# Output projection in seven products: the bank for the products of block sums comes from another pair of places

## The chip, the cores and the metric

The kernel runs on one core of one Trainium2 chip. The metric is the device time of one execution in microseconds (us), lower being better. Engines are named as in the profile: PE is TensorE (PEld its weight loads), DVE is VectorE, ACT is ScalarE, POOL is GpSimd and SP is SyncE, which here only issues transfers.

## The reference

One layer of a hybrid encoder on 256 tokens of width 2048. Eight heads do softmax attention with forget gates (group A), eight do stick-breaking attention (group B). Each group's output is normalised over its 1024 columns, both are multiplied by `w_out` and added to the input, and a convolutional feed-forward follows. The change lies in the product with `w_out`:

```
D_MODEL = 2048; SEQ = 256; HEAD_DIM = 128; N_HEADS_FOX = N_HEADS_SB = 8
def hybrid_mixer(h, ...):
    proj = h @ w_in_l
    ...
    out_a = forgetting_attention(qa, ka, to_heads(va, N_HEADS_FOX), c)
    out_b = stick_breaking_attention(...)
    merged = jnp.concatenate([rms_norm(from_heads(out_a), out_norm_fox_l),
                              rms_norm(from_heads(out_b), out_norm_sb_l)], axis=-1)
    return merged @ w_out_l

def reference(...):
    h = rms_norm(x, attn_norm);  x = x + hybrid_mixer(h, ...)
    h = rms_norm(x, ffn_norm);   x = x + conv_ffn(h, ...)
```

## The kernel before

**Precision and splits.** All large products are made of float32 operands that are split into a high and a low part. `split` (L220, L221) does it for weights: ACT casts the raw 128x2048 tile into `w_hi`, and DVE subtracts to get `w_lo`. A product is then high x high, high x low and low x high: `in_three` (L245) issues, for one bank and four blocks of 128 rows, eight matmuls with `w_hi` and then four with `w_lo`. `w_hi` and `w_lo` have two buffers each in this stage, the raw tiles three, so that the split for a product waits until PE is through with the product two before it, and the load of a raw tile until the split of the tile three before it is done.

**The output projection.** For 256 tokens it makes two kinds of products. `token_major` makes plain ones for both halves of the tokens together: an `acc` tile of two banks, with 16 matmuls of `w_hi` and 8 of `w_lo` for each load of weights. For the heads of group A and the last 1024 columns, `in_seven` makes a 2x2 block product in seven products rather than eight, from sums of blocks of the operand (`oT_blocks`, split into `oT_sums`) and sums of blocks of the weights (`w_sum` and `x12`, to which POOL's transfers add other blocks in memory, L848). `in_seven` is a generator: `token_major` takes one step of it after each of its loads, so that on PE plain products alternate with products of the seven.

**Banks.** The seven products land in three accumulators: `bank_a` (products 1, 5, 6, 7), `bank_c` (product 2) and `bank_b` (products 3 and 4). After each product `residual` (L833) multiplies the bank by a factor for each token and adds it to the running `x` on DVE. PSUM places come from pools. `pss` has two places with tag "s", which the heads used for scores and transposed weights (`ps_s`, `ps_z`, `ps_p`). `psb` has two places with tag "t", which hold the heads' products with the values (`ps_o`), the sums over heads (`pg`, L919) and the transposes of the next stage (`ps_x`, L146). `psa` has the two `acc` tiles. With `bank_a` in use until the seventh product, `bank_b` gets the place that `bank_c` had.

**Order.** PE's instructions stand in program order. Those of DVE, ACT, POOL and SP are ordered by a scheduler, which follows the dependences and the priorities that the code gives; each engine then runs its list in that order.

The stage of interest lies between 325 and 400 us of the profiled execution. Its products on PE, in order, are called here: K1 (plain, group B, first columns, first half), B1 (`bank_b`, first of two), K2 (plain, second half), B2 (`bank_b`, second), `pg`, K3 (plain, next columns), A1 (`bank_a` from `w_sum`).

Of the kernel before, what the change touches and what calls it, by code (L numbers as in the profile page):

```python
# [9 lines left out]
F32 = mybir.dt.float32  # L10
# [5 lines left out]
P = 128  # L16
# [30 lines left out]
def hybrid_layer(  # L47
# [29 lines left out]
    psb = ctx.enter_context(tc.tile_pool(name="psb", bufs=2, space=bass.MemoryType.PSUM))  # L77
# [135 lines left out]
    def split(raw, a, b):  # L213
        hi = whi.tile([P, 2048], F32R, name="w_hi", tag="w_hi")
        lo = wlo.tile([P, 2048], F32R, name="w_lo", tag="w_lo")
        n = a * b
        with ExitStack() as turn:
            for ins in in_turn:
                turn.enter_context(tc.issue_after(ins.ins))
            last = [act.copy(hi[:, :n], raw[:, :n])]  # L220
            last.append(dve.tensor_tensor(lo[:, :n], raw[:, :n], f32(hi[:, :n]), op=ALU.subtract))  # L221
        last_split[:] = last
        if in_turn:
            in_turn[:] = last
        return (
            hi[:, :n].rearrange("p (a b) -> p a b", a=a),
            lo[:, :n].rearrange("p (a b) -> p a b", a=a),
        )

    def weights(src, a, b):  # L230
        with tc.high_priority(offset=AHEAD):
            return split(load(src), a, b)

    def rows_of(w, k0, n, c0, cols):
        return w[k0 * P : (k0 + n) * P, c0 : c0 + cols].rearrange("(k p) c -> p k c", p=P)

    def in_three(accs, parts, n, lhs, starts, stops, more=False):

        hi, lo = parts
        order = [(i, l, hi) for i in range(n) for l in range(2)] + [(i, 0, lo) for i in range(n)]
        for j, (i, l, r) in enumerate(order):
            for t, o in enumerate(accs):
                nc.tensor.matmul(  # L245
                    o, lhs(i, l, t), r[:, i, :], start=starts and j == 0,
                    stop=stops and j == 3 * n - 1, skip_group_check=more,
                )

    def of_half(h, part, t):  # L250
        return h[:, part, t * P : (t + 1) * P]
# [52 lines left out]
    with ExitStack() as actx:  # L304

        at = actx.enter_context(tc.tile_pool(name="at", bufs=1))
        pss = actx.enter_context(tc.tile_pool(name="pss", bufs=2, space=bass.MemoryType.PSUM))
# [487 lines left out]
        def block_parts():  # L795
            sums.extend(big.tile([P, NH, S], F32R, name="oT_sums", tag=f"hT{g}") for g in (1, 2))
            places = [[t[:, 4 * h : 4 * h + 4] for t in sums] for h in range(2)]
            for (hi, _), block in zip(places, blocks):
                in_order(act.copy(hi, block))
            for (hi, lo), block in zip(places, blocks):  # L800
                in_order(dve.tensor_tensor(lo, block, f32(hi), op=ALU.subtract))
# [29 lines left out]
        def residual(t, c, ps, factor):  # L831
            xs = xt[t][:, c : c + 512]
            dve.scalar_tensor_tensor(xs, ps, factor[:, t : t + 1], xs, op0=ALU.mult, op1=ALU.add)  # L833

        def in_seven(c0, plus_rg, minus_rg):

            w11, w12, w21, w22 = (rows_of(wo, 4 * h, 4, c0 + 512 * i, 512) for h in range(2) for i in range(2))
            banks = {}

            def of_heads(h, t):  # L840
                return lambda i, part, _: of_half(oT[4 * h + i], part, t)

            def of_sums(h, t):
                return lambda i, part, _: sums[part][:, 4 * h + i, t * P : (t + 1) * P]

            def plus(into, src):
                with tc.high_priority(offset=AHEAD):
                    nc.gpsimd.dma_start(  # L848
                        into.rearrange("p (a b) -> p a b", a=4), src, accum_op=ALU.add
                    )  # L850

            def product(bank, lhs, parts, to, factor=plus_rg):
                new = bank not in banks
                if new:
                    banks[bank] = pss.tile([P, 512], F32, name=bank, tag="s")
                in_three([banks[bank]], parts, 4, lhs, new, True, more=not new)
                residual(to[0], c0 + 512 * to[1], banks[bank], factor)

            w, x12 = (
                pool.tile([P, 2048], F32, name=name, tag=tag)  # L860
                for pool, name, tag in ((at, "w_sum", "vA"), (big, "x12", "hT0"))
            )
            with tc.high_priority(offset=AHEAD):
                for into, src in ((w, w11), (x12, w12)):
                    nc.sync.dma_start(into.rearrange("p (a b) -> p a b", a=4), src)
            yield
            yield
            yield
            with tc.issue_after(last_head[0].ins), tc.issue_after(last_head[1].ins):
                parts = split(w, 4, 512)  # L870
                in_order(dve.tensor_tensor(w, w, x12, op=ALU.add))
                block_parts()
            product("bank_a", of_heads(0, 0), parts, (0, 0))
            product("bank_c", of_heads(1, 0), weights(w21, 4, 512), (0, 0))
            yield
            with tc.high_priority(offset=AHEAD):
                parts = split(w, 4, 512)
            plus(w, w22)
            plus(x12, w22)
            product("bank_b", of_sums(0, 1), parts, (1, 1))  # L880
            yield
            product("bank_b", of_sums(1, 0), weights(w22, 4, 512), (0, 1))
            yield
            with tc.high_priority(offset=AHEAD):
                parts = split(w, 4, 512)
            plus(w, w21)
            product("bank_a", of_sums(1, 1), parts, (0, 1), minus_rg)
            yield
            with tc.high_priority(offset=AHEAD):
                parts = split(x12, 4, 512)  # L890
            product("bank_a", of_sums(0, 0), parts, (1, 1), minus_rg)
            yield
            with tc.high_priority(offset=AHEAD):
                parts = split(w, 4, 512)
            product("bank_a", of_heads(1, 1), parts, (1, 0))
# [405 lines left out]
```

## Time and profile before

| | |
|---|---|
| median of 3 runs | 1106.46 us (1105.9 to 1107.39) |
| the profiled execution's own time | 1107.04 us |
| its span | 1105.2 us |
| PE busy | 1096.8 us, 99% of the span |
| DVE / ACT / POOL busy | 895.3 / 709.0 / 47.9 us |
| mean granted clock of TensorE | 0.997 |
| moved by DMA | 249.04 MB, mean 225 GB/s |

The span runs from the first to the last instruction of the program; the execution takes 1.84 us beyond it. The chain that ended last is PE for 99% of the span. Busy time on PE counts matmuls at whatever clock was granted, so a stretch at half clock counts as busy and takes twice as long.

### The profile page before, as it was taken

How to read it: one execution, taken by the hardware profiler on the slowest of the kernel's cores; microseconds unless marked ns; L12 is line 12 of the kernel's file. 1: busy time of each engine (PE TensorE's matmuls, PEld its weight loads, DVE VectorE, ACT ScalarE, POOL GpSimd, SP SyncE). 2: the span in 40 equal slices, each digit the busy share in tenths (PEclk: the TensorE clock that was granted, in tenths of full speed). 3: DMA queues.
4: the chain of work that ended last, by engine and by line, in shares of the span. 5: the costliest groups of instructions: out<-in, count | busy, mean ns of one | idle time of the engine just before them, and what ended most of it. 6: DMA issues, size and time to landing. Idle time of an engine off the chain costs nothing.

```text
span 1105.2 us, 14835 instructions
## 1 busy us (share of the span) xinstructions
PE 1096.8 (99%) x5856; PEld 950.9 (86%) x5856; DVE 895.3 (81%) x957; ACT 709.0 (64%) x884; POOL 47.9 (4%) x49
## 2 busy tenths in 40 slices
PE   9999999999998999999999999999999999999998
PEld 7998888888887888888888888888888888888887
DVE  6656778877787777689889888889798888889896
ACT  6544555764673667677767776667676777577753
POOL 0000000000000000000000010100000010100010
PEclk9999999999998999999999999999999999999999
DMA  8776554676648495557989597986979689987975
GB/s 288 185 232 231 186 153 152 195 239 205 205 126 250 114 306 196 191 189 189 308 205 327 191 225 259 267 261 183 313 212 302 214 223 283 237 261 204 323 203 181
DMA packets 180991, 249.04 MB, mean 225 GB/s; under 512 B 4480, under 2 KB 119066, under 8 KB 180666
## 3 DMA queue, kind: packets, MB, share of 16 engines
q1 hardware_dynamic: 162458, 209.67, 57.7%
q0 software_dynamic: 18144, 37.89, 18.2%
q8 instruction: 46, 0.75, 0.3%
q10 hardware_dynamic: 320, 0.53, 0.1%
q14 instruction: 23, 0.19, 0.0%
HBM read 245.97 MB, written 2.11 MB: 224 GB/s over the span
## 4 chain that ended last, share of the span: by engine, by line
PE 99%; DVE 0%; DMA 0%; issue 0%; SPq 0%
PE pu L271 34%; PE acc L245 20%; PE pu L277 18%; PE bank_a L245 11%; PE bank_b L245 6%; PE bank_c L245 3%; PE acc L446 2%; PE acc L1179 1%; PE ps_x L146 1%; PE ps_o L612 1%; PE bank_a L1179 1%; PE ps_p L628 0%; DMA w_raw<-in_w_in_dram 0%; PE ps_o L613 0%; PE ps_h L324 0%; PE ps_s L540 0%
## 5 line engine op out<-in xcount | busy, mean ns | idle before, releaser
L221 DVE TENSOR_TENSOR w_lo<-w_raw,w_hi 128x2048 fp32r<-128x2048 f32 (+1 forms) x194 | 434.9, 2245 | 123.0 <-ACT w_hi L220 122.1
L220 ACT CAST w_hi<-w_raw 128x2048 fp32r<-128x2048 f32 (+1 forms) x194 | 363.5, 1876 | 229.3 <-PE acc L245 63.4
L271 PE MATMUL pu<-hT,w_hi 128*128 128x512 f32 x1664 | 394.0, 390 | 0.0
L271 PEld LDWEIGHTS pu<-hT,w_hi 128*128 128x128 f32 x1664 | 310.3, 188 | 63.1
L277 PEld LDWEIGHTS pu<-hT,w_lo 128*128 128x128 f32 x1664 | 211.9, 191 | 7.0
L277 PE MATMUL pu<-hT,w_lo 128*128 128x256 f32 x1664 | 215.2, 283 | 0.0
L245 PE MATMUL acc<-w_hi,hT 128*128 128x512 f32 (+1 forms) x576 | 124.5, 368 | 0.0
L245 PEld LDWEIGHTS acc<-w_hi,hT 128*128 128x128 f32 x576 | 101.9, 188 | 14.6
L221 DVE TENSOR_TENSOR w_lo<-w_sum,w_hi 128x2048 fp32r<-128x2048 f32 x34 | 77.8, 2290 | 21.6 <-ACT w_hi L220 21.6
L220 ACT CAST w_hi<-w_sum 128x2048 fp32r<-128x2048 f32 x34 | 64.9, 1909 | 44.8 <-PE pu L271 36.7
L996 ACT ACTIVATE tap<-up,ccol 128x256 f32<-128x256 f32 x176 | 74.6, 495 | 0.0
L245 PE MATMUL acc<-w_lo,hT 128*128 128x512 f32 (+1 forms) x288 | 64.6, 366 | 0.0
L245 PEld LDWEIGHTS acc<-w_lo,hT 128*128 128x128 f32 x288 | 51.6, 188 | 7.5
L1101 POOL DMA_DIRECT2D w_sum<-in_w_down_dram x20 | 25.4, 1272 | 678.5 <-DVE w_lo L221 665.4
L245 PE MATMUL bank_a<-w_hi,s 128*128 128x512 f32 x160 | 40.0, 392 | 0.0
L245 PE MATMUL bank_a<-w_hi,g 128*128 128x512 f32 x160 | 40.0, 392 | 0.0
L245 PE MATMUL bank_b<-w_hi,s 128*128 128x512 f32 x160 | 40.0, 392 | 0.0
L245 PEld LDWEIGHTS bank_a<-w_hi,g 128*128 128x128 f32 x160 | 28.9, 189 | 5.3
L245 PEld LDWEIGHTS bank_a<-w_hi,s 128*128 128x128 f32 x160 | 28.9, 189 | 5.3
L245 PEld LDWEIGHTS bank_b<-w_hi,s 128*128 128x128 f32 x160 | 28.9, 189 | 5.3
L1078 DVE TENSOR_TENSOR x<-x,bank_a 128x512 f32<-128x512 f32 (+1 forms) x43 | 28.8, 669 | 4.4 <-PE bank_a L1179 3.8
L1001 DVE TENSOR_TENSOR gate<-gate,tap 128x512 f32<-128x512 f32 x44 | 30.3, 688 | 2.5 <-ACT tap L996 0.2
(248 smaller groups left out, 1112.6 us busy)
## 6 DMA issues: line engine op xcount, KB each, us to landing
w_raw<-in_w_up_dram SPq DMA_DIRECT2D x88, 1024.0 KB, 7.7
w_raw<-in_w_down_dram SPq DMA_DIRECT2D x44, 1024.0 KB, 6.5
w_raw<-in_w_in_dram SPq DMA_DIRECT2D x36, 1024.0 KB, 5.3
w_sum<-in_w_down_dram POOLq DMA_DIRECT2D x20, 1024.0 KB, 10.5
w_raw<-in_w_out_dram SPq DMA_DIRECT2D x14, 1024.0 KB, 5.3
w_raw<-in_w_down_dram POOLq DMA_DIRECT2D x10, 1024.0 KB, 14.5
w_raw<-in_w_in_dram SPq DMA_DIRECT2D x12, 688.0 KB, 4.0
w_raw<-in_w_in_dram SPq DMA_DIRECT2D x6, 512.0 KB, 6.9
```

Source lines behind the costliest of these rows:

```text
L146: nc.tensor.transpose(ps[:, j, t * P : (t + 1) * P], xt[t][:, (k + j) * P : (k + j + 1) * P], ident)
L220: last = [act.copy(hi[:, :n], raw[:, :n])]
L221: last.append(dve.tensor_tensor(lo[:, :n], raw[:, :n], f32(hi[:, :n]), op=ALU.subtract))
L245: nc.tensor.matmul(o, lhs(i, l, t), r[:, i, :], start=starts and j == 0, stop=stops and j == 3 * n - 1, skip_group_check=more,)
L271: nc.tensor.matmul(acc[:, j, :], hi[:, i, j * P : (j + 1) * P], hT[k].rearrange("p a b -> p (a b)"), start=k == 0, stop=low_first and k == ...
L277: nc.tensor.matmul(acc[:, j, S:], lo[:, i, j * P : (j + 1) * P], hT[k][:, 0, :], start=False, stop=not low_first and k == KT - 1,)
L446: nc.tensor.matmul(acc[:, t, :], of_half(hT[2 * c + i + j], l, t), r[:, j, :], start=high and c == i == m == 0, stop=not high and c == 7 a ...
L996: act.activation(taps[w][:, j, :], u[:, j, w : w + S], AF.Copy, scale=ccol[:, w, f : f + 1])
L1001: dve.tensor_tensor(a, a, tap, op=ALU.add)
L1078: dve.tensor_tensor(xs, xs, ps, op=op)
L1101: nc.gpsimd.dma_start(mem[into][:, : nk * 512].rearrange("p (a b) -> p a b", a=nk), src, accum_op=ALU.add)
L1179: nc.tensor.matmul(o, of_half(g, l, t), r[:, i, c0 : c0 + cols], start=kh == 0 and j == 0, stop=kh == n - 1 and j == 11,)
```

## The change

The bank of products 3 and 4, `bank_b`, is taken from `psb` (tag "t"). The other two stay in `pss`.

```
             def product(bank, lhs, parts, to, factor=plus_rg):
                 new = bank not in banks
                 if new:
-                    banks[bank] = pss.tile([P, 512], F32, name=bank, tag="s")
+                    pool, tag = (psb, "t") if bank == "bank_b" else (pss, "s")
+                    banks[bank] = pool.tile([P, 512], F32, name=bank, tag=tag)
                 in_three([banks[bank]], parts, 4, lhs, new, True, more=not new)
                 residual(to[0], c0 + 512 * to[1], banks[bank], factor)
```

No operation is added or removed, and the lists of ACT, POOL and SP, with their waits, are the same. On PE the order of the matmuls is the same too; what differs is what they wait for. PE's list from the last matmuls of K1 (`acc` from `oT`) to B2, before:

```order
L245 MATMUL acc<-w_lo,oT_2254 128x512 x2
L245 MATMUL bank_b<-w_hi,oT_sums 128x512 [waits DVE_49,Activation_49]
L245 MATMUL bank_b<-w_hi,oT_sums 128x512 x7
L245 MATMUL bank_b<-w_lo,oT_sums 128x512 x4
L245 MATMUL acc<-w_hi,hT_79 128x512 [waits Activation_49]
L245 MATMUL acc<-w_hi,hT_79 128x512 x15
L245 MATMUL acc<-w_lo,hT_79 128x512 x8
L245 MATMUL bank_b<-w_hi,oT_sums 128x512 [waits DVE_49,Activation_49]
```

and after:

```order
L245 MATMUL acc<-w_lo,oT_2254 128x512 x2
L245 MATMUL bank_b<-w_hi,oT_sums 128x512 [waits Activation_49]
L245 MATMUL bank_b<-w_hi,oT_sums 128x512 x7
L245 MATMUL bank_b<-w_lo,oT_sums 128x512 [waits DVE_49]
L245 MATMUL bank_b<-w_lo,oT_sums 128x512 x3
L245 MATMUL acc<-w_hi,hT_79 128x512 [waits Activation_49]
L245 MATMUL acc<-w_hi,hT_79 128x512 x15
L245 MATMUL acc<-w_lo,hT_79 128x512 [waits DVE_49]
L245 MATMUL acc<-w_lo,hT_79 128x512 x7
L245 MATMUL bank_b<-w_hi,oT_sums 128x512 [waits DVE_49,Activation_49]
```

The wait on DVE in front of B1's first matmul is gone. The low parts of B1 and K2 wait for DVE by themselves now; before, that one wait had covered them. B2 waits for DVE in both.

On DVE the scheduler moved one split. The rows run from the residual of `bank_c` to that of the second product in `bank_b`; the first `w_lo` split in them is that of B2's weights, the second that of K3's:

```order
 L833 SCALAR_TENSOR_TENSOR x_2954<-bank_c,rg_2832,x_2954 128x512 [waits DVE_49]
-L833 SCALAR_TENSOR_TENSOR x_2954<-acc,rg_2832,x_2954 128x512 x2
-L833 SCALAR_TENSOR_TENSOR x_2954<-bank_b,rg_2832,x_2954 128x512 [waits PE_49]
-L221 TENSOR_TENSOR w_lo<-w_raw,w_hi 128x2048 [waits DMAHW2_49,Activation_49]
+L833 SCALAR_TENSOR_TENSOR x_2954<-acc,rg_2832,x_2954 128x512
+L221 TENSOR_TENSOR w_lo<-w_raw,w_hi 128x2048 [waits DMAHW2_49,PE_49,Activation_49]
+L833 SCALAR_TENSOR_TENSOR x_2954<-acc,rg_2832,x_2954 128x512
+L833 SCALAR_TENSOR_TENSOR x_2954<-bank_b,rg_2832,x_2954 128x512
 L221 TENSOR_TENSOR w_lo<-w_raw,w_hi 128x2048 [waits DMAHW3_49,PE_49,Activation_49]
 L833 SCALAR_TENSOR_TENSOR x_2954<-bank_b,rg_2832,x_2954 128x512 [waits PE_49]
```

The split of B2's weights stood behind the residual of B1; it now stands two places ahead of it, between the two residuals of an earlier `acc`.

More of the change, by code (lines that the diff above doesn't have):

```diff
@@ L854, in product @@
                 if new:
-                    banks[bank] = pss.tile([P, 512], F32, name=bank, tag="s")
+                    pool, tag = (psb, "t") if bank == "bank_b" else (pss, "s")
+                    banks[bank] = pool.tile([P, 512], F32, name=bank, tag=tag)
                 in_three([banks[bank]], parts, 4, lhs, new, True, more=not new)
```

## The prediction

> **What bounds the kernel now.** I read the page first, then who waited for whom on PE, then the timelines of PE, DVE and ACT around the one long wait, and last the granted clock there. The page's first part and PE's list of waits (us in total, times, longest):
>
> ```profile
> span 1105.2 us, 14835 instructions
> PE 1096.8 (99%) x5856; PEld 950.9 (86%) x5856; DVE 895.3 (81%) x957; ACT 709.0 (64%) x884; POOL 47.9 (4%) x49
> ...
> PE bank_b L245 <- DVE x L833: 3.6, 1, 3.6
> PE idle L399 <- DVE zeros L389: 1.1, 1, 1.1
> PE acc L446 <- DVE w_hi L427: 0.5, 1, 0.5
> ```
>
> PE is the bound from end to end. It waits three times, two of them in the opening. The only wait in the body is one of 3.6 us before `bank_b`, for a residual (L833) on DVE. So whatever moves PE's products after it earlier arrives at the end in full, unless a new wait appears. PE's timeline there (start, length, instructions, idle before):
>
> ```profile
> 331.24 3.79 PE L245 MATMUL acc<-w_hi,oT 128*128 128x512 f32 x16
> 334.87 1.97 PE L245 MATMUL acc<-w_lo,oT 128*128 128x512 f32 x8
> 340.42 3.75 PE L245 MATMUL bank_b<-w_hi,oT_sums 128*128 128x512 f32 x8 [3.58 <-DVE x L833]
> 343.97 1.91 PE L245 MATMUL bank_b<-w_lo,oT_sums 128*128 128x512 f32 x4
> 345.68 3.94 PE L245 MATMUL acc<-w_hi,hT 128*128 128x512 f32 x16
> 349.45 1.98 PE L245 MATMUL acc<-w_lo,hT 128*128 128x512 f32 x8
> 351.26 1.98 PE L245 MATMUL bank_b<-w_hi,oT_sums 128*128 128x512 f32 x8
> 353.08 1.07 PE L245 MATMUL bank_b<-w_lo,oT_sums 128*128 128x512 f32 x4
> 353.99 0.50 PE L919 MATMUL pg<-cs,ssq 128*128 128x1 f32 x4
> 354.35 3.93 PE L245 MATMUL acc<-w_hi,oT 128*128 128x512 f32 x16
> ...
> 359.93 1.98 PE L245 MATMUL bank_a<-w_hi,oT_sums 128*128 128x512 f32 x8
> ```
>
> In order these are K1, B1, K2, B2, `pg`, K3 and A1. Besides the wait, see B1's length: the same twelve matmuls take 340.42 to 345.68 = 5.26 us in B1, and 351.26 to 353.99 = 2.73 in B2. The granted clock by half microseconds (stretch, length, busy times, clock, DMA share, GB/s) says why:
>
> ```profile
> 338.50:339.00 0.50, 0.00 (x0) 0.00 (x0) 0.50 (x1) 0.00 (x0) 0.00 (x0) 1.00 1.07 381
> 339.00:339.50 0.50, 0.00 (x0) 0.00 (x0) 0.50 (x1) 0.00 (x0) 0.00 (x0) 0.56 1.14 319
> ...
> 340.50:345.00 4.50, 4.50 (x11) 3.53 (x12) 1.09 (x2) 0.79 (x1) 0.00 (x0) 0.50 1.11 232
> ...
> 345.50:346.00 0.50, 0.50 (x2) 0.38 (x2) 0.08 (x1) 0.50 (x1) 0.00 (x0) 0.61 1.10 262
> ```
>
> The clock is halved at about 339.06 (0.56 over the half microsecond) and full again at about 345.6. The wait thus costs its own length and, by the halved clock, most of B1 a second time.
>
> What did PE wait for? DVE's timeline:
>
> ```profile
> 328.54 0.87 DVE L375 SCALAR_TENSOR_TENSOR hT<-ps_o,pcol,hT 128x256 fp32r<-128x256 f32 x2
> ...
> 332.66 2.29 DVE L221 TENSOR_TENSOR w_lo<-w_sum,w_hi 128x2048 fp32r<-128x2048 f32 x1
> ...
> 335.20 1.22 DVE L801 TENSOR_TENSOR oT_sums<-oT_blocks,oT_sums 128x1024 fp32r<-128x1024 f32 x1
> ...
> 337.33 2.28 DVE L221 TENSOR_TENSOR w_lo<-w_raw,w_hi 128x2048 fp32r<-128x2048 f32 x1
> 339.53 0.74 DVE L833 SCALAR_TENSOR_TENSOR x<-bank_c,rg,x 128x512 f32<-128x512 f32 x1
> 340.19 1.40 DVE L833 SCALAR_TENSOR_TENSOR x<-acc,rg,x 128x512 f32<-128x512 f32 x2
> 345.92 0.75 DVE L833 SCALAR_TENSOR_TENSOR x<-bank_b,rg,x 128x512 f32<-128x512 f32 x1 [4.33 <-PE bank_b L245]
> ```
>
> The residual of `bank_c` ends at 339.53 + 0.74 = 340.27, and PE goes on at 340.42. `bank_c` was complete when K1 began (331.24), but DVE first worked through its list. B1 had to wait since its bank is `bank_c`'s place.
>
> **The change, term by term.** *The wait.* K1 takes 334.87 - 331.24 = 3.63 for its high part and, as K2 does (349.45 to 351.26), 1.81 for the low one, so PE is free for B1 at 331.24 + 3.63 + 1.81 = 336.68. Are B1's inputs there, and the new place? ACT's timeline:
>
> ```profile
> 329.63 0.64 ACT L382 ACTIVATE osq<-ps_o 128x256 f32<-128x256 f32 x2
> 330.59 1.92 ACT L220 CAST w_hi<-w_sum 128x2048 fp32r<-128x2048 f32 x1 [0.32 <-PE bank_c L245]
> 335.06 1.91 ACT L220 CAST w_hi<-w_raw 128x2048 fp32r<-128x2048 f32 x1 [2.56 <-PE acc L245]
> 344.21 1.90 ACT L220 CAST w_hi<-w_raw 128x2048 fp32r<-128x2048 f32 x1 [7.24 <-PE bank_b L245]
> ...
> 353.28 1.91 ACT L220 CAST w_hi<-w_sum 128x2048 fp32r<-128x2048 f32 x1 [1.71 <-PE bank_b L245]
> ```
>
> The new place was last held by a head's `ps_o`, whose readers end at 329.63 + 0.64 = 330.27 (ACT) and 328.54 + 0.87 = 329.41 (DVE): 6.4 us to spare. B1's `w_hi` is there at 330.59 + 1.92 = 332.51, its `w_lo` at 332.66 + 2.29 = 334.95. So B1 starts at 336.68 in place of 340.42: **3.74 us**.
>
> *The clock.* Without the wait PE has no idle time in which the clock could fall, and B1 takes B2's 2.73 in place of 5.26: **2.53 us**. K2 then starts at 339.41 in place of 345.68, **6.27 us** earlier in all.
>
> The Trainium skill, "TensorE: Matmul & The Clock Gate", Part 1 (The HAM clock gate), says that the clock is halved after at least one idle window of about 3.4 us, and that the window runs freely. The trace differs in one point: here the clock fell 339.06 - 336.84 = 2.2 us after PE's last matmul ended. For the whole removal both give the same sum; for a wait that is only shortened to between 2.2 and 3.4 us, the page keeps the 2.53 us and this trace does not promise them.
>
> *What is late next.* K2's `w_hi` is there at 335.06 + 1.91 = 336.97, before 339.41, and its `w_lo` at 337.33 + 2.28 = 339.61, before its low part at 339.41 + 3.77 = 343.18 (3.77 from 345.68 to 349.45). B2 is the thin place. It is due at 339.41 + 5.58 = 344.99 (5.58 from 345.68 to 351.26), and must find its weights split and B1's residual done, for it goes on in the same bank. Its weights' issue and landing (KB, us to landing), and those of the transfer that adds to `w_sum`, with the page's row of the slowest such transfers:
>
> ```profile
> 328.65 0.37 SPq L208 DMA_DIRECT2D w_raw<-in_w_out_dram  x1
> ...
> w_raw<-in_w_out_dram SPq DMA_DIRECT2D x1, 1024.0 KB, 9.6
> ...
> 335.25 1.27 POOL L848 DMA_DIRECT2D w_sum<-in_w_out_dram  x1 [6.93 <-DVE w_lo L221]
> ...
> w_sum<-in_w_out_dram POOLq DMA_DIRECT2D x1, 1024.0 KB, 12.5
> ...
> w_raw<-in_w_down_dram POOLq DMA_DIRECT2D x10, 1024.0 KB, 14.5
> ```
>
> B2's weights land at 328.65 + 9.6 = 338.25. The cast needs the buffer that B1's high part frees at 336.68 + 1.82 = 338.50 (1.82 from 351.26 to 353.08); ACT follows 0.24 later, as before (343.97 to 344.21), from 338.74 to 340.64. DVE goes through `bank_c` (to 340.19), one `acc` residual (0.66 by the distance 339.53 to 340.19, so to 340.85), B2's split (2.20 by the distance 337.33 to 339.53, to 343.05), the other `acc` residual (to 343.71) and B1's residual (0.75, to 344.46). With the 0.15 that PE took to react, B2 could start at 344.61, and PE comes at 344.99: **0 us, with 0.38 to spare**. The moved split is what makes it thin: it is queued ahead of B1's residual, and behind it wait that residual and, through it, PE. Should the weights land later than about 338.9, each us costs one.
>
> A1 needs the sum in `w_sum`, which lands at 335.25 + 12.5 = 347.75, since that transfer's start hangs on a split at 334.95 which doesn't move. ACT would take it up at 344.99 + 1.82 + 0.20 = 347.01 (0.20 as from 353.08 to 353.28), waits until 347.9 and is done at 349.8. PE comes to A1 at 344.99 + 2.73 + 0.36 + 5.58 = 353.66 (`pg`: 353.99 to 354.35; K3: 354.35 to 359.93): 3.9 us to spare. From there all lists and distances are those of before, where PE never waited again.
>
> *Sum.* 1107.04 (the profiled execution, 1105.2 of it the span) - 6.27 = 1100.77. The profiled execution lies 0.58 above the median of 1106.46; against the median the sum is **1100.2 us**.
>
> **The rivals.** *The half clock is not in the shown runs* (0.05). The clock's fall depends on when its measure was taken, and in runs without a profile it may be absent; then only 3.74 is to be had, 1102.7 us. Against it: the shown runs lie within 1.49 us of each other and the profiled one between them, less than the 2.53 that would separate runs with and without it.
>
> *B2 waits a little* (0.07). By the thin 0.38 above; a landing up to 2.2 us later than 338.9 gives 1100.2 to 1102.4. For it: DMA is busy all the time (share above 1 in the clock's rows). Against it: up to 336.68 nothing has moved, so the landing is that of before.
>
> *Slower: B2's weights land so late that the moved split holds up B1's residual and PE for longer than PE waited before* (0.03). At the slowest transfer's 14.5 us they land at 343.15; cast, split and two residuals follow in 344.61 - 338.74 = 5.87 plus 0.25, so B2 starts at 349.27, a wait of 4.28, over which the clock falls again (2.53). That loses 6.81 where 6.27 was gained: 1107.0 us. It decides from a landing of about 342.6 on, and each us beyond 343.15 adds one; slower by over 0.2% begins at about 344.8.
>
> *No change: the weights' transfers are the real limit and PE only changes what it waits for* (0.02): 1106.5 us. `w_sum` would have to land 10.1 us later than at 347.75 (3.9 to spare and 6.27), but PE's list of waits has none for a transfer or a split. The Trainium skill has such a case, "TensorE: Matmul & The Clock Gate", Part 1 (HAM oscillation): a matmul kernel in which double-buffering PSUM gave no further gain. No run here shows that; PE's 3.58 us behind a PSUM reader speak against it.
>
> That the change doesn't do what it says can be left out: PE's list after it has no wait on DVE ahead of B1.
>
> **How the numbers follow.** The whole sum has a chance of 0.83, its own range 1099.0 to 1101.2: the shown runs (1105.9 to 1107.39) less 6.27 give 1099.6 to 1101.1, and the lower end goes 0.6 further, in case the half clock reached into K2 in some shown runs (1.2 us of K2 at half clock). The range reaches up to the two nearest rivals, 1102.7. Of the measurement's 0.2%, about 2.2 us, the whole sum, the little wait and the missing half clock are all faster, 0.95; within it lie no change and two thirds of the slower case, whose price at 14.5 us is 0.5, 0.04; slower is the last third, 0.01.
>
> **What would show it.** In the profile after, PE's list of waits has no `bank_b` row; B1 starts at about 336.7 and takes 2.7; the clock stays at 1.00 through 325 to 400 us; the cast of `w_sum` waits a little for its transfer; the span is about 1098.9. I am wrong if B2 or A1 shows a wait on DVE or ACT, if the clock is halved elsewhere, or if PE's later products are no longer 6.27 us earlier than before.

## The result and the profile after

The changed kernel takes 1101.19 us (median of 6 runs, 1100.61 to 1102.19) against 1106.85 us before (6 runs, 1105.9 to 1109.28). The ratio is 0.9947, with a 95% interval of 0.9934 to 0.996: 5.7 us or 0.5% faster. All six runs after have a mean granted clock of 1.000. The profiled execution took 1100.61 us, its span 1098.8.

The page's first rows after:

```profile
span 1098.8 us, 14833 instructions
...
PE 1094.2 (100%) x5856; PEld 949.3 (86%) x5856; DVE 895.2 (81%) x957; ACT 709.3 (65%) x884; POOL 47.9 (4%) x49
...
PEclk9999999999999999999999999999999999999999
```

The span lost 6.4 us, but PE's busy time lost only 2.6. A wait removed shortens the span; a stretch at half clock that is removed shortens the busy time too. PE's list of waits after (us in total, times, longest):

```profile
PE idle L399 <- DVE zeros L389: 1.1, 1, 1.1
PE acc L446 <- ACT hT L151: 0.3, 1, 0.3
```

The `bank_b` row is gone and none has come in its place; both rows left are in the opening. PE's timeline from the end of K1 to the start of K3:

```profile
334.86 1.98 PE L245 MATMUL acc<-w_lo,oT 128*128 128x512 f32 x8
336.67 1.98 PE L245 MATMUL bank_b<-w_hi,oT_sums 128*128 128x512 f32 x8
338.48 1.07 PE L245 MATMUL bank_b<-w_lo,oT_sums 128*128 128x512 f32 x4
339.39 3.79 PE L245 MATMUL acc<-w_hi,hT 128*128 128x512 f32 x16
343.01 1.98 PE L245 MATMUL acc<-w_lo,hT 128*128 128x512 f32 x8
344.83 1.98 PE L245 MATMUL bank_b<-w_hi,oT_sums 128*128 128x512 f32 x8
346.64 1.07 PE L245 MATMUL bank_b<-w_lo,oT_sums 128*128 128x512 f32 x4
347.55 0.50 PE L920 MATMUL pg<-cs,ssq 128*128 128x1 f32 x4
```

B1 starts at 336.67 and takes 2.72 us. B2 starts at 344.83 where it started at 351.26, 6.43 earlier. DVE and ACT show how narrowly B2 is served. DVE from `bank_c`'s residual on:

```profile
339.52 0.75 DVE L833 SCALAR_TENSOR_TENSOR x<-bank_c,rg,x 128x512 f32<-128x512 f32 x1
340.18 0.75 DVE L833 SCALAR_TENSOR_TENSOR x<-acc,rg,x 128x512 f32<-128x512 f32 x1
340.84 2.29 DVE L221 TENSOR_TENSOR w_lo<-w_raw,w_hi 128x2048 fp32r<-128x2048 f32 x1
343.03 0.75 DVE L833 SCALAR_TENSOR_TENSOR x<-acc,rg,x 128x512 f32<-128x512 f32 x1
343.69 0.75 DVE L833 SCALAR_TENSOR_TENSOR x<-bank_b,rg,x 128x512 f32<-128x512 f32 x1
```

`bank_c`'s residual still ends at 340.27; now nobody waits for it. B1's residual ends at 343.69 + 0.75 = 344.44, 0.39 ahead of B2. Before the change PE started 0.15 after the residual that it waited for (340.27 to 340.42); with that time taken off, 0.24 is to spare. ACT's casts of B2's weights and of `w_sum`:

```profile
338.68 1.91 ACT L220 CAST w_hi<-w_raw 128x2048 fp32r<-128x2048 f32 x1 [1.71 <-PE bank_b L245]
...
347.40 1.91 ACT L220 CAST w_hi<-w_sum 128x2048 fp32r<-128x2048 f32 x1 [2.27 <-DMA w_sum<-in_w_out_dram]
```

The cast of `w_sum` waits for its transfer now, as forecast, and is done at 349.31, long before A1.

### The profile page after: what moved, and what is told of

Its sections match the earlier page's. It is cut to its first block, busy times and chain, and to the rows that moved or that the text cites. A ratio compares the mean times of both kernels' runs of the same rounds, so it can differ in the third digit from the quotient of the medians.

```text
span 1098.8 us, 14833 instructions
## 1 busy us (share of the span) xinstructions
PE 1094.2 (100%) x5856; PEld 949.3 (86%) x5856; DVE 895.2 (81%) x957; ACT 709.3 (65%) x884; POOL 47.9 (4%) x49
## 4 chain that ended last, share of the span: by engine, by line
PE 100%; ACT 0%; DVE 0%; issue 0%
PE pu L271 34%; PE acc L245 20%; PE pu L277 18%; PE bank_a L245 11%; PE bank_b L245 5%; PE bank_c L245 3%; PE acc L446 2%; PE acc L1180 1%; PE ps_x L146 1%; PE ps_o L612 1%; PE bank_a L1180 1%; PE ps_p L628 0%; PE ps_o L613 0%; PE ps_h L324 0%; PE idle L399 0%; PE ps_s L540 0%
## 5 line engine op out<-in xcount | busy, mean ns | idle before, releaser
L1002 DVE TENSOR_TENSOR val<-val,tap 128x512 f32<-128x512 f32 x44 | 30.3, 688 | 2.3
```

Source lines behind the costliest of these rows:

```text
L1002: dve.tensor_tensor(a, a, tap, op=ALU.add)
```

## The experiments

The theory: PE waited because B1's bank was the place that a reader on DVE had not left. The gain is that wait plus the halved clock behind it; the moved split has no part in it.

**The wait kept, PE kept busy in it.** On the kernel before, matmuls on zeros fill the wait:

```
+            filler = psb.tile([P, S], F32, name="filler", tag="t")
+            for _ in range(28):
+                nc.tensor.matmul(filler, zeros[:, :P], zeros, start=True, stop=True)
             product("bank_b", of_sums(0, 1), parts, (1, 1))
```

> The kernel before, with 28 matmuls on zeros (256 columns, never read) put on PE ahead of B1, some 3 us of work inside the 3.58 us wait. The wait for bank_c's residual stays; only the idleness goes. Theory (the wait costs 3.74 us and the halved clock 2.5 to 2.7 us apart from it): B1 still starts at about 340.4, the clock stays at 1.00, B1 takes 2.73 in place of 5.26, and the run is 2.5 to 2.7 us faster than before, about 1104.2. Rival (the wait alone is the cost, the halved clock delays nothing that matters): the time of before, 1106.9.

1104.6 us (12 runs, 1104.19 to 1104.86) against 1106.56; ratio 0.9978, 0.997 to 0.9986. Its PE timeline:

```profile
336.75 3.23 PE L882 MATMUL filler<-zeros 128*128 128x256 bf16 x28
340.50 2.08 PE L245 MATMUL bank_b<-w_hi,oT_sums 128*128 128x512 f32 x8 [0.52 <-DVE x L833]
342.41 1.07 PE L245 MATMUL bank_b<-w_lo,oT_sums 128*128 128x512 f32 x4
343.32 3.79 PE L245 MATMUL acc<-w_hi,hT 128*128 128x512 f32 x16
```

B1 starts as late as before but takes 2.8 us, and the mean clock is 0.999 or 1.000 in all twelve runs. So the half clock is a cost of its own, about 2.0 us in the median. From here to the changed kernel and to the next run are 3.4 and 3.5 us, the wait. The rival, that the length alone counts, falls.

**The residual earlier, the places as before.** On the kernel before, the first residuals of `bank_a` and `bank_c` get a high priority:

```
-                residual(to[0], c0 + 512 * to[1], banks[bank], factor)
+                first = new and bank != "bank_b"
+                with tc.high_priority(offset=AHEAD) if first else nullcontext():
+                    residual(to[0], c0 + 512 * to[1], banks[bank], factor)
```

> The places as before; instead the residuals of bank_a and bank_c get a high priority, so that DVE runs them as soon as the banks are complete and not behind two splits. Theory (the wait is for the reader of the place, not for the place as such): B1 finds bank_c's place free at 336.7, and the run takes about 1101.2, as the changed kernel. Rival (the shared place costs something of its own): between 1101.2 and 1106.9.

1101.08 us (6 runs); ratio 0.9945, 0.9932 to 0.9959: the changed kernel's gain without its change. On DVE the residual of `bank_c` comes ahead of the split for B1:

```profile
332.21 0.74 DVE L833 SCALAR_TENSOR_TENSOR x<-bank_c,rg,x 128x512 f32<-128x512 f32 x1
332.88 2.28 DVE L221 TENSOR_TENSOR w_lo<-w_sum,w_hi 128x2048 fp32r<-128x2048 f32 x1
```

It ends at 332.95 and not at 340.27, and PE has no wait. A shared place costs nothing when its reader is through in time.

**The moved split put back.** On the changed kernel, the residual of B1 is put ahead of B2's split (`in_turn` lists the instructions that the next split has to follow; that `residual` and `product` now return theirs is not shown):

```
-            product("bank_b", of_sums(0, 1), parts, (1, 1))
+            first = product("bank_b", of_sums(0, 1), parts, (1, 1))
             yield
+            in_turn.append(first)
```

> The changed kernel, with DVE's list put back as it was before the change: the split of B2's weights stands behind B1's residual again. Theory (the gain is the place alone, and the moved split has nothing to do with it): B1's residual ends about 2.2 us earlier than in the changed kernel, the split after it, both in time for B2, no wait on PE; the time of the changed kernel, about 1101.2. Rival (the moved split brings part of the gain): 0.5 us or more slower, with a wait at B2.

1100.96 us (5 runs); ratio 0.9951, 0.9937 to 0.9964. On DVE the residual of B1 is through before the split of B2's weights starts:

```profile
340.52 1.40 DVE L833 SCALAR_TENSOR_TENSOR x<-acc,rg,x 128x512 f32<-128x512 f32 x2
341.84 0.74 DVE L833 SCALAR_TENSOR_TENSOR x<-bank_b,rg,x 128x512 f32<-128x512 f32 x1
342.50 2.28 DVE L221 TENSOR_TENSOR w_lo<-w_raw,w_hi 128x2048 fp32r<-128x2048 f32 x1
```

PE's list has no wait but those of the opening. The moved split is not part of the gain.

**The other bank moved.** On the changed kernel:

```
-                    pool, tag = (psb, "t") if bank == "bank_b" else (pss, "s")
+                    pool, tag = (psb, "t") if bank == "bank_c" else (pss, "s")
```

> The other way round: bank_c comes from the pair of psb and bank_b from the pair of pss, so that again no two of the three share a place. DVE's list keeps the split of B2's weights behind B1's residual, as before the change. Theory (what counts is that B1 does not wait for bank_c's residual, whichever place is moved): the time of the changed kernel, about 1101.2, and no wait on PE at B1 or B2. Rival (the moved split on DVE gives part of the gain): slower than the changed kernel by 0.5 us or more, with a wait at B2.

1102.67 us (7 runs); ratio 0.9966, 0.9952 to 0.998. Neither: 1.5 us slower than the changed kernel, by a wait that no theory had. PE's list has it, and ACT's timeline shows for whom (times in this execution are 2.2 us later from the opening on):

```profile
PE bank_c L245 <- ACT osq L382: 1.4, 1, 1.4
```

```profile
329.99 1.91 ACT L220 CAST w_hi<-w_raw 128x2048 fp32r<-128x2048 f32 x1 [1.37 <-PE bank_a L245]
331.81 0.64 ACT L382 ACTIVATE osq<-ps_o 128x256 f32<-128x256 f32 x2
```

The place in `psb` was last held by a head's `ps_o`, and its last reader on ACT stands behind a cast. `bank_c` follows the heads after one product of PE and has to wait; `bank_b` comes 8 us later, when that reader is through.

**A shorter wait.** On the kernel before, K2's split is queued behind `bank_c`'s residual (`ahead`, empty at first, holds it; that `residual` returns its instruction is not shown):

```
+                r = residual(to[0], c0 + 512 * to[1], banks[bank], factor)
+                if bank == "bank_c":
+                    ahead.append(r)
+                elif bank == "bank_b" and new:
+                    in_turn.extend(ahead)
```

> The places as before; on DVE the residual of bank_c goes ahead of the split of K2's weights, behind one acc residual. By DVE's list it ends at 338.7 in place of 340.3, so that PE waits 2.0 us in place of 3.58. Theory by the trace of before (there the clock fell 2.2 us after the last matmul, so a wait of 2.0 us is too short): the clock stays, 1.5 + 2.6 = 4.1 us faster than before, about 1102.7. Rival (a wait of 2.0 us halves the clock as well): only 1.5 us faster, 1105.3.

1104.7 us (12 runs, 1102.73 to 1105.44); ratio 0.9975, 0.9965 to 0.9985. The wait is 2.04 us as reckoned, but my expectation on the clock failed. Three runs have a mean granted clock of 0.999 or 1.000 and times of 1102.73 to 1103.37; nine have 0.998 and 1104.45 to 1105.44. The profiled one is of the nine. Its PE timeline and its granted clock (stretch, length, busy times, clock, DMA share, GB/s):

```profile
339.12 2.60 PE L245 MATMUL bank_b<-w_hi,oT_sums 128*128 128x512 f32 x8 [2.04 <-DVE x L833]
```

```profile
340.00:340.25 0.25, 0.25 (x3) 0.21 (x2) 0.25 (x1) 0.00 (x0) 0.00 (x0) 1.00 1.14 270
340.25:340.50 0.25, 0.25 (x3) 0.21 (x2) 0.25 (x1) 0.00 (x0) 0.00 (x0) 0.94 1.02 270
340.50:340.75 0.25, 0.25 (x3) 0.14 (x2) 0.25 (x1) 0.00 (x0) 0.00 (x0) 0.50 1.16 262
...
343.75:344.00 0.25, 0.25 (x3) 0.21 (x1) 0.25 (x1) 0.00 (x0) 0.00 (x0) 0.73 1.16 213
```

The clock fell at 340.47 (0.94 of its quarter microsecond), 1.35 us after PE had gone on, and rose at 343.88 (0.73): 3.41 us. Before the change it was low twice as long, 6.83 us, from 339.06 to 345.89, by the quarters in which it fell (0.62) and rose (0.72):

```profile
339.00:339.25 0.25, 0.00 (x0) 0.00 (x0) 0.25 (x1) 0.00 (x0) 0.00 (x0) 0.62 0.98 295
...
345.75:346.00 0.25, 0.25 (x2) 0.22 (x1) 0.08 (x1) 0.25 (x1) 0.00 (x0) 0.72 1.10 262
```

**Longer waits.** The same kernel with n additions on DVE (never read) ahead of `bank_c`'s residual, n = 3 and n = 9:

```
+                if bank == "bank_c":
+                    xs = xt[to[0]][:, c0 : c0 + S]
+                    for _ in range(n):
+                        spare = tmp.tile([P, S], F32, name="spare", tag="t1", bufs=3)
+                        dve.tensor_tensor(spare, xs, xs, op=ALU.add)
```

> The kernel of the shorter wait, with three additions of 128x256 (never read) on DVE ahead of bank_c's residual, which moves it by some 1.0 us, so that PE waits about 3.0 us, less than the whole window of 3.4 us that the Trainium skill states. Theory (a window that is idle for the greater part is enough): the clock falls in most runs, by one window of 3.4 us, which costs 1.7; with 3.0 + 0.1 for the wait over the changed kernel's 1101.2 that makes 1104.3 in a run without a fall and 1106.0 in one with it. Rival (the page's rule, one whole idle window): no fall, 1104.3 and a mean clock of 1.000 in all runs.

> The same with nine additions: PE waits about 5.1 us, longer than before the change. Theory (wait and half clock add up): the clock falls in every run, the wait costs 5.2 over 1101.2 and the half clock 1.7 to 2.6 on the work after it: 1108.1 to 1109.0, about 1.5 to 2.5 slower than the kernel before. Rival (the half clock depends on the wait's length, so that a longer wait costs more of it): over 1110.

With three: 1107.3 us (11 runs); ratio 1.0005, 0.9996 to 1.0014. The wait was 3.7 us and not 3.0, since the scheduler put a second `acc` residual ahead of `bank_c`'s, which I had not counted. PE's list of waits and DVE's timeline:

```profile
PE bank_b L245 <- DVE x L833: 3.7, 1, 3.7
```

```profile
338.35 1.08 DVE L861 TENSOR_TENSOR spare<-x 128x256 f32<-128x256 f32 x3
339.35 0.74 DVE L833 SCALAR_TENSOR_TENSOR x<-acc,rg,x 128x512 f32<-128x512 f32 x1
340.01 0.74 DVE L833 SCALAR_TENSOR_TENSOR x<-bank_c,rg,x 128x512 f32<-128x512 f32 x1
```

So it does not test a wait under the 3.4 us of the expectation. With nine the wait is 5.7 us for the same reason:

```profile
PE bank_b L245 <- DVE x L833: 5.7, 1, 5.7
```

1109.24 us (10 runs); ratio 1.0023, 1.0014 to 1.0033, all with a mean clock of 0.997. Wait and half clock add up: 1101.2 + 5.7 + 0.15 leaves 2.2 for the clock. Above the changed kernel, waits of 2.04, 3.7 and 5.7 us cost 3.5, 6.1 and 8.0. Beside the wait itself that is 1.5, where three runs of twelve had no fall, then 2.4 and 2.3: from 3.7 to 5.7 us of wait the half clock costs no more.

**The spare time of B2.** On the changed kernel, three such additions ahead of B1's residual:

```
+                if bank == "bank_b" and new:
+                    xs = xt[to[0]][:, c0 + 512 * to[1] : c0 + 512 * to[1] + S]
+                    for _ in range(3):
+                        spare = tmp.tile([P, S], F32, name="spare", tag="t1", bufs=3)
+                        dve.tensor_tensor(spare, xs, xs, op=ALU.add)
```

> The changed kernel, with three additions of 128x256 (never read) on DVE ahead of B1's residual. They take 1.0 us, and the scheduler then also puts the split of K3's weights ahead of that residual; that split has to wait for a cast that starts when K2's high part ends, at 343.2. So B1's residual ends at about 348.1 in place of 344.4. Theory (B2 waits for B1's residual and had 0.4 us to spare): a wait of 3.3 us at B2, 1101.2 + 3.3 = 1104.5 in a run without a fall of the clock, 1.7 to 2.6 more with it, about 1106.5 in all: nearly the whole gain given back. Rival (B2 has more room than reckoned): no wait, 1101.2.

1106.55 us (11 runs, 1103.91 to 1108.23); ratio 0.9998, 0.9988 to 1.0007: the whole gain is gone. PE's list of waits and DVE's timeline:

```profile
PE bank_b L245 <- DVE x L833: 3.3, 1, 3.3
```

```profile
343.66 1.08 DVE L862 TENSOR_TENSOR spare<-x 128x256 f32<-128x256 f32 x3
345.11 2.29 DVE L221 TENSOR_TENSOR w_lo<-w_raw,w_hi 128x2048 fp32r<-128x2048 f32 x1 [0.36 <-ACT w_hi L220]
347.32 0.74 DVE L833 SCALAR_TENSOR_TENSOR x<-bank_b,rg,x 128x512 f32<-128x512 f32 x1
```

One microsecond of work in the wrong place moved a split of 2.29 us, with a wait for ACT, ahead of the residual that PE needs. Eight of the eleven runs have a mean clock of 0.998 or less, though the wait is shorter than 3.4 us. The profiled run, at 1105.36, is one of the other three (1.000). Its list of waits also has 0.7 us in three places further on, before `bank_a` (L1084), so not all that it lost was lost at B2.

## Why the prediction was right, and where not

**The wait** was forecast at 3.74 us. The profiles have 340.42 - 336.67 = 3.75, and the run with the clock held puts it at 3.4 to 3.5 in the medians and, by its profiled execution of 1104.39, at 3.78. The residual in front, the free place, B1's inputs: all as the steps said. By the runs with an early residual and with the split put back, the cause is shown: a reader of the place that comes too late.

**The clock** was forecast at 2.53. In the profiles B1 went from 5.26 to 2.72, which is 2.54, and K2 from 5.58 to 5.44 (339.39 to 344.83). That 0.14 I had missed: the step "5.58 from 345.68 to 351.26" took its price from a K2 whose first 0.2 us still ran at half clock. I had read the clock as full again at about 345.6, but a mean of 0.61 over 345.5 to 346.0 means half clock up to 345.89. So B2 came at 344.83 and not at 344.99, and 6.43 us were gained in the profile, 1107.04 to 1100.61, where the sum said 1100.77. As PE came earlier, the 0.38 to spare at B2 was 0.24.

**From the profile to the median** is the step that failed. I took the 0.58 us by which the profiled execution lay above its median as a constant and subtracted it again: 1100.2. The measured median is 1101.19, and the profiled execution after lies 0.58 *below* it. Of the 0.99 us between them, 0.39 is the median before, 1106.46 in three runs and 1106.85 in six. The rest is the gain: 5.66 between the medians where I had 6.27.

The mean clocks give a reason. Of the 50 runs of the kernel before that stand beside the experiments, 5 have a mean clock of 1.000 and a median of 1104.59, 29 have 0.998 and 1106.4, 16 have less. A stretch of 3.41 us at half clock takes 3.41 x 0.5 / 1105 = 0.0015 off the mean, one of 6.83 us 0.003. So the commonest run pays for one such stretch, at most 1.7 us, and the profiled one (0.997) had paid 2.54 + 0.14 for two. With one stretch the gain would be 3.75 + 1.7, about 5.5. That this is the reason is argued and not shown: the interval of the result reaches from 4.4 to 7.3 us and holds both gains.

**The rivals.** "The half clock is not in the shown runs" was true for 5 of 50 runs and false for the median. "B2 waits a little" did not come: the forecast had B1's residual end at 344.46, the profile 344.44. The slower case did not come either, but its mechanism is real: in the last experiment a split ahead of B1's residual, K3's and late by a cast rather than by a transfer, gave the whole gain back. The case in which transfers are the real limit fell: the cast of `w_sum` waited 2.27 us and PE none.

## What to carry to other kernels

A PSUM place is free when its last reader has run (at 340.27 here), not when its accumulation ends (at 331.24); so look at where that reader stands in its engine's list, and either give the next accumulator a place whose reader is long done, or move the reader up (both gave the same 5 to 6 us here, and the place of the heads' products was good for the later bank only). Where a wait on TensorE is removed, price the half clock apart from the wait, from the runs' mean clock rather than from one profile. After such a change look for the operation with the least time to spare: 0.24 us here, and one microsecond of work on DVE, which drew a split ahead of the residual, undid the gain.

## What the runs showed of the hardware

The clock fell after waits shorter than I had thought possible, and later than I had thought. A wait of 2.04 us halved it in 9 of 12 runs, one of 3.27 us in 8 of 11; one of 1.37 us left the mean clock at 1.000 in all 7 runs. (Each wait is read from one profiled execution, the falls from the mean clock of every run.) The fall can come when PE is busy again (1.35 us after, above), and the half clock held for 3.41 or 6.83 us. After the last matmul before the wait, the fall came 2.2 us later in the kernel before and 3.4 us later in the run above.

That fits a window of about 3.4 us that runs freely, as the Trainium skill has it ("TensorE: Matmul & The Clock Gate", Part 1). It does not fit the same page's condition of at least one idle window: in the run above the 3.41 us up to the fall, 337.06 to 340.47, hold 2.04 us of idleness and 1.35 of matmuls, and no other 3.41 us there hold more of the wait than its 2.04. Where the limit lies between 1.37 and 2.04 us, and whether it is one of the share of a window, stays open.

Part of the scatter goes with the clock. Over its 50 runs the kernel before is spread from 1104.37 to 1110.53, with medians of 1104.59, 1106.4 and 1107.9 at mean clocks of 1.000, 0.998 and less; with the clock held by filler matmuls, 12 runs lay within 0.7 us. That the phase of the window decides how many stretches a run pays for is argued from these mean clocks, not shown run by run. Another part does not show in the clock: with the other bank moved all 7 runs have 1.000 and lie between 1102.3 and 1104.94. In the profiled one, at 1104.31, the first eight matmuls of 512 columns took far longer than in the changed kernel's profile. The changed kernel's come first here:

```profile
6.03 2.09 PE L446 MATMUL acc<-w_hi,hT 128*128 128x512 f32 x8 [0.31 <-ACT hT L151]
```

```profile
6.57 3.73 PE L446 MATMUL acc<-w_hi,hT 128*128 128x512 f32 x8 [0.23 <-DVE w_hi L427]
```

From there on that execution is 2.2 us later, and its rows of the granted clock read 1.00 in the opening. So a run can lose time in the opening that its mean clock does not tell; why is not shown.
